# A two-layer convolution and attention trunk: the issue order of every engine written out in traced order

## The chip, the cores and the metric

The kernel runs on one core of a Trainium2 chip. The metric is device time in microseconds for one execution of the whole program, and the kernel before has a median of 1953.31 us over 3 runs (1951.56 to 1954.4). In the text PE is the matmul engine, DVE the vector engine, ACT the scalar engine, POOL the GpSimd engine (here it issues DMAs) and SP the engine that issues the weight loads.

## What is computed

There are 256 tokens with 2048 channels, in float32, and two layers. A layer is this:

```python
h = rmsnorm(x, norm_g)
c_a, c_glu, c_gate, q_down, kv_down, k_pe, m_gate, g_conv, g_mla = split(h @ w_in)
u = causal_depthwise_conv(c_a * sigmoid(c_glu), width=31) + conv_b
y_conv = (silu(layernorm(u)) * silu(c_gate)) @ w_proj_conv
q = rmsnorm(q_down) @ w_uq;  kv = rmsnorm(kv_down) @ w_ukv     # 16 heads, QK norm, rotary part
y_mla = (chunk_causal_attention(q, k, v) * silu(m_gate)) @ w_proj_mla
x = x + (sigmoid(g_conv) * y_conv + sigmoid(g_mla) * y_mla) @ w_out
```

## The kernel before, in words

Every dense product takes float32 weights and activations split in a high and a low part. ACT casts the weights to the high part, `hi` (line 198), DVE subtracts it to get the low part, `lo` (line 199), and PE runs three matmuls per tile: hi with the activations' high part, lo with it, hi with their low part (lines 251 to 253). Weights come by SP in pieces of four 128-row tiles (`load`, line 177, three buffers). A piece makes two splits of two tiles each (`split`, line 189, three buffers each for hi and lo). One split feeds 12 matmuls: two token halves, two tiles, three terms. This text calls that stretch of PE work a slot. `product` (line 239) is the loop over the slots of one block of output columns: for slot i it first issues split i+2, then the 12 matmuls, then `background` (line 216). A block has 16 tiles (8 slots) or, for `uq` and `ukv`, 4 tiles (2 slots); it is 512 columns wide, except `down` (384, 384, 320) and `uq` (384).

`order_of_layer` (line 88) sets the order of the blocks: three `down` blocks, two `glu` blocks, then for each of 8 pairs of heads one `uq`, one `ukv` and one `glu` (or `cgate`) block; then `cgate`, `mgate`, `gmla`, `pmla`, `gconv`, `pconv`, `wout`, four blocks each.

Work beside the products: `attention` (line 532) places the steps of a pair of heads a given number of slots ahead (constants at lines 64 and 65). `turn` (line 281) transposes a tile through DRAM: POOL writes it out with four DMAs, fetches it back `FETCH_AFTER` slots later, DVE transposes 32x32 blocks. `conv` (line 703) puts the 31 taps of a channel block on the list `fill`, each two DVE instructions (line 715). `layernorm` (line 727) puts its steps there too: `centre` subtracts the mean and squares, `var` computes the factor 1/sqrt, `apply` multiplies by it on DVE and runs Silu on ACT, `gated` transposes the gate, multiplies, and splits the result (`ycT`) on ACT and DVE. `background` takes from `fill` at a rate; what is left is drained at the first `pconv` block (line 948). The results of `mgate`, `pconv` and `wout` go through `turn` and are split on ACT and DVE too (`oT` lines 826 and 827, `yT` lines 806 and 807, `hT` lines 897 to 900).

What decides the order on each engine: the Tile framework's scheduler, which runs on a timeline of its own. The wrappers `vec`, `act` and `dma` (line 126) pin the order among the instructions issued through them; instructions issued with `nc.vector`, `nc.scalar`, `nc.tensor` and `nc.sync` are free. Splits are issued with a high priority (line 197), and some steps are tied behind the newest split (lines 203 and 580).

Of the kernel before, what the change touches and what calls it, by code (L numbers as in the profile page):

```python
# [2 lines left out]

# [8 lines left out]
F32 = mybir.dt.float32  # L12
# [46 lines left out]
N_WARM = 9  # L59
TURNED_AFTER = 7  # L60
FETCH_AFTER = 4


STATS_AT, QK_OUT_AT, QK_BACK_AT, ROPE_AT, NOPE_AT, SCORES_AT = 1, 4, 8, 13, 14, 17
P_OUT_AT, P_BACK_AT, P_AT, VALUES_AT = 20, 24, 28, 30

SUMS_AFTER = 1
# [20 lines left out]
def order_of_layer():  # L88

    order = [("down", i, "win") for i in range(len(DOWN_BLOCKS))] + [("glu", 0, "win"), ("glu", 1, "win")]  # L90
    for b in range(NPAIR):
        order += [("uq", b, "wuq"), ("ukv", b, "wukv")]
        if b + 2 < 8:
            order.append(("glu", b + 2, "win"))
        elif b + 1 < NPAIR:
            order.append(("cgate", 0, "win"))
    for kind, s in (
        ("cgate", "win"), ("mgate", "win"), ("gmla", "win"), ("pmla", "wpm"),
        ("gconv", "win"), ("pconv", "wpc"), ("wout", "wo"),
    ):  # L100
        order += [(kind, i, s) for i in range(1 if kind == "cgate" else 0, 4)]
    return order
# [11 lines left out]
def trunk(ctx: ExitStack, tc: tile.TileContext, xT, x, g_in, pos, win, wuq, wukv, wpc, wpm, wo, cst, rows, invf, out):  # L114
    nc = tc.nc

    class InOrder:


        def __init__(self, engine):  # L120
            self.engine = engine

        def __getattr__(self, name):
            return lambda *a, **k: tc.keep_in_program_order(getattr(self.engine, name)(*a, **k))  # L124

    vec, act, dma = InOrder(nc.vector), InOrder(nc.scalar), InOrder(nc.gpsimd)
# [45 lines left out]
    loaded, done, newest = {}, {}, [None]  # L172
    deferred = deque()
    LOAD_AHEAD, SPLIT_AHEAD = 2, 2
    SPLIT_SOONER = 100

    def load(i):
        if i >= len(pieces) or i in loaded:
            return
        ap, n = pieces[i]  # L180
        t = raw_p.tile([P, KG, n], F32, tag="raw", name=f"raw{i}")
        step = KS if i == 0 else KG
        for k in range(0, KG, step):
            if i == 0:
                load_x(k // step)
            nc.sync.dma_start(t[:, k : k + step, :], ap[:, k : k + step, :])
        loaded[i] = t

    def split(i):
# [7 lines left out]
        with tc.high_priority(offset=SPLIT_SOONER):  # L197
            nc.scalar.copy(hi, r)  # L198
            ins = nc.vector.tensor_sub(lo, r, hi.bitcast(F32))  # L199
        done[i] = hi, lo  # L200
        newest[0] = ins.ins
        while deferred and deferred[0][0] <= i:
            with tc.issue_after(ins.ins):
                deferred.popleft()[1]()
# [4 lines left out]
    attn, fill = deque(), deque()  # L209
    budget = {"fill": 0.0, "rate": 0.0, "slots": 0}  # L210
    steps, clock = [], [0]

    def at_slot(ahead, f):
        steps.append((clock[0] + ahead, f))

    def background():
        clock[0] += 1
        if attn:
            attn.popleft()()
        due = [f for slot, f in steps if slot <= clock[0]]  # L220
        steps[:] = [e for e in steps if e[0] > clock[0]]
        for f in due:
            f()
        if budget["slots"]:

            budget["rate"] = max(sum(cost for cost, _ in fill), 0.0) / budget["slots"]
            budget["slots"] -= 1
        budget["fill"] = min(budget["fill"] + budget["rate"], 4.0)
        while fill and budget["fill"] > 0:
            cost, f = fill.popleft()  # L230
            budget["fill"] -= cost
            f()

    def drain(q):
        while q:
            f = q.popleft()
            (f[1] if isinstance(f, tuple) else f)()

    def product(planned, stat, evacuate):
        nk, n, mine = planned  # L240
        pts = [acc_p.tile([P, 512], F32, tag="acc", name=f"acc{mine[0]}_{t}") for t in range(T)]
        for j, i in enumerate(mine):
            for a in range(SPLIT_AHEAD + 1):
                split(i + a)
            hi, lo = done[i]
            for t in range(T):
                for kk in range(KS):
# [3 lines left out]
                    nc.tensor.matmul(pts[t][:, :n], sh, hi[:, kk, :], start=first, stop=False)  # L251
                    nc.tensor.matmul(pts[t][:, :n], sh, lo[:, kk, :], start=False, stop=False)  # L252
                    nc.tensor.matmul(pts[t][:, :n], sl, hi[:, kk, :], start=False, stop=last)  # L253
            if j < len(mine) - 1:
                background()
        for t in range(T):
            evacuate(t, pts[t][:, :n])
        background()
# [5 lines left out]
    def park(src, n, home):  # L264
        d = home.tile([4, 32, 4, n // 4], F32, tag=f"t{n}", name="turn_d")
        for i in range(4):
            dma.dma_start(
# [5 lines left out]
    def fetch(d, z):  # L273
        dma.dma_start(z, d.rearrange("j s i e -> (j s) (i e)"))
# [6 lines left out]
    def turn(src, n, use, dst=None):  # L281
# [4 lines left out]
        at_slot(FETCH_AFTER, lambda: back.append(fetched(d, n)))  # L286
# [6 lines left out]
        deferred.append((len(done) - 1 + TURNED_AFTER, blockwise))  # L293
# [24 lines left out]
    nc.vector.memset(ones, 1.0 / D)  # L318
# [7 lines left out]
    nc.vector.memset(zeros.bitcast(F32), 0.0)  # L326
    nc.scalar.copy(sin2[:, 0, 0, :], ones[:, :HALF])
    warm = tp_p.tile([P, 512], F32, tag="tp", name="warm")
    for i in range(N_WARM):
        nc.tensor.matmul(warm, zeros[:, :P], zeros, start=i == 0, stop=i == N_WARM - 1)  # L330

    gains = const.tile([P, DEPTH, NCT], F32, name="gains")
    nc.sync.dma_start(gains, g_in)
    x_in = big.tile([P, NCT, SEQ], F32, tag="big", name="x_in")
    x_chunks = [(0, 2), (2, 4), (4, 8), (8, 12), (12, 16)]

    def load_x(i):
        a, b = x_chunks[i]
        nc.sync.dma_start(x_in[:, a:b, :], xT[:, a:b, :])

    def rope_tables():
        invf_t = const.tile([P, HALF], F32, name="invf_t")
        nc.gpsimd.dma_start(invf_t, invf.partition_broadcast(P))
        pos_t = const.tile([P, T], I32, name="pos_t")
        nc.gpsimd.dma_start(pos_t, pos)
        posf = const.tile([P, T], F32, name="posf")
        nc.vector.tensor_copy(posf, pos_t)
        tables = wide_p.tile([P, 6, T, HALF], F32, tag="w", name="tables")
        ang, ah, al, turn, whole, frac = (tables[:, i] for i in range(6))
        ah = ah.bitcast(F32R)  # L350
        for t in range(T):
            nc.vector.tensor_scalar(ang[:, t, :], invf_t, posf[:, t : t + 1], None, op0=ALU.mult)
        nc.vector.tensor_copy(ah, ang)
        nc.vector.tensor_sub(al, ang, ah.bitcast(F32))
        big_half = 1.5 * 2.0**23

        def reduce_to(dst, src, scale):

            nc.vector.tensor_scalar(whole, src, scale, big_half, op0=ALU.mult, op1=ALU.add)
            nc.vector.tensor_scalar(whole, whole, -big_half, None, op0=ALU.add)  # L360
            nc.vector.scalar_tensor_tensor(dst, src, scale, whole, op0=ALU.mult, op1=ALU.subtract)

        first = True
        for piece in revolution_pieces():
            for a in (ah.bitcast(F32), al):
                reduce_to(turn if first else frac, a, piece)
                if not first:
                    nc.vector.tensor_add(turn, turn, frac)
                first = False
        for dst, shift in ((sin2, 0.0), (cos2, 0.25)):  # L370
            nc.vector.tensor_scalar(frac, turn, shift, None, op0=ALU.add)
            reduce_to(ang, frac, 1.0)
            for h in range(2):
                nc.scalar.activation(dst[:, :, h, :], ang, AF.Sin, scale=2.0 * np.pi)
# [4 lines left out]
    def sum_x():  # L379
        tot = small.tile([P, T], F32, tag="totx", name="totx")  # L380
        nc.vector.reduce_sum(tot, ss_x, axis=AX.X)
# [5 lines left out]
    load(0)  # L387
    for i in range(2, len(x_chunks)):
        load_x(i)
        if i < len(x_chunks) - 1:  # L390
            load(i - 1)
    for c in range(NCT):
        g = gains[:, 0, c : c + 1]
        nc.scalar.activation(h_hi[:, c, :], x_in[:, c, :], AF.Copy, scale=g)
        nc.vector.scalar_tensor_tensor(
            h_lo[:, c, :], x_in[:, c, :], g, h_hi[:, c, :].bitcast(F32), op0=ALU.mult, op1=ALU.subtract
        )

    def first_sums(t, c):
        xt = wide_p.tile([P, 512], F32, tag="w", name="xres")  # L400
        tc.keep_in_program_order(nc.sync.dma_start(xt, x[t, :, c * 512 : (c + 1) * 512]))
        junk = work.tile([P, 512], F32, tag="junk", name="junk")
        nc.scalar.activation(junk, xt, AF.Square, accum_out=ss_x[:, t, c : c + 1])


    for l in range(DEPTH):
# [9 lines left out]
        def load_consts(row=row, C=C, l=l):  # L416
            tc.keep_in_program_order(nc.sync.dma_start(row, rows[l].partition_broadcast(P)))
            tc.keep_in_program_order(nc.sync.dma_start(C, cst[l]))
# [9 lines left out]
        def down_evac(i, t, ps, down=down):  # L428
            at, n = DOWN_BLOCKS[i]
            nc.scalar.activation(down[:, t, at : at + n], ps, AF.Copy, scale=rinv_x[:, t : t + 1])  # L430

        def down_after(down=down, qkc=qkc, ss_d=ss_d, r_d=r_d, kpe=kpe, ccq=ccq, ssq_t=ssq_t, gqk=gqk, row=row, C=C):
            for t in range(T):
                for i, (a, n) in enumerate(((0, LORA), (LORA, LORA), (2 * LORA, ROPE))):
                    junk = work.tile([P, 512], F32, tag="junk", name="junk")
                    nc.scalar.activation(junk[:, :n], down[:, t, a : a + n], AF.Square, accum_out=ss_d[:, i, t : t + 1])
            rms_factor(r_d.rearrange("p a t -> p (a t)"), ss_d[:, 0:2, :].rearrange("p a t -> p (a t)"), LORA)
            for i in range(2):
                for t in range(T):
                    d = down[:, t, i * LORA : (i + 1) * LORA]  # L440
                    nc.vector.scalar_tensor_tensor(
                        d, d, r_d[:, i, t : t + 1], row[:, i * LORA : (i + 1) * LORA], op0=ALU.mult, op1=ALU.mult
                    )
            for c in range(0, 8, 2):
                tp = tp_p.tile([P, 2, SEQ], F32, tag="tp", name="tp_d")
                for j in range(2):
                    for t in range(T):
                        nc.tensor.transpose(
                            tp[:, j, t * P : (t + 1) * P], down[:, t, (c + j) * P : (c + j + 1) * P], ident
                        )  # L450
                nc.scalar.copy(qkc[:, 0, c : c + 2, :], tp)
                nc.vector.tensor_sub(qkc[:, 1, c : c + 2, :], tp, qkc[:, 0, c : c + 2, :].bitcast(F32))

            def gained(dst, table, base):
                g = row[:, base : base + ROPE].unsqueeze(1).broadcast_to([P, T, ROPE])
                nc.vector.tensor_mul(dst, table.rearrange("p t h d -> p t (h d)"), g)
# [599 lines left out]
```

## Time and profile before

| what | value |
| --- | --- |
| the profiled execution's own time | 1953.72 us |
| its span, first to last instruction | 1952.0 us |
| around the span | 1.7 us |
| median of the three timed runs | 1953.31 us |
| DMA | 437.58 MB, mean 224 GB/s |
| ACT busy | 1111.4 us (57%) |
| POOL busy | 363.0 us (19%) |

In a row of a group the columns are: line, engine, operation, names out<-in, shapes, count; then busy time and mean length of one in ns; then the idle time of the engine just before them and what ended it. In a timeline row: start, length, engine, line, operation, names, shape, count, and in brackets the engine's idle time before it. A length counts until the result has left the pipeline, so two independent instructions on one engine start a little closer together than a length.

### The profile page before, as it was taken

The page shows a single profiled execution, that of the slowest core. Times are in us where ns is not written, and L with a number is a line of the kernel's source. Part 1 is how long each engine was busy: PE and PEld are TensorE (multiplying, and loading weights), DVE is VectorE, ACT ScalarE, POOL GpSimd, SP SyncE. Part 2 cuts the span into 40 slices and gives each one's busy share as a digit, 9 for nine tenths or more (in the row PEclk, how much of TensorE's full clock was granted, in tenths as well). Part 3 has the DMA queues.
Part 4 walks back from the last instruction along what each step waited for, and adds up shares of the span by engine and source line. Part 5 has one row for each costly group of instructions (what it writes and reads, how often), then busy time and mean ns, then how long its engine had stood idle before and what let it go on. Part 6 is the DMA issues. An engine that isn't in the chain of part 4 may idle for free.

```text
span 1952.0 us, 25418 instructions
## 1 busy us (share of the span) xinstructions
PE 1910.5 (98%) x8781; PEld 1607.7 (82%) x8781; DVE 1614.0 (83%) x2884; ACT 1111.4 (57%) x1778; POOL 363.0 (19%) x684
## 2 busy tenths in 40 slices
PE   9999999999999999999999999999999999999998
PEld 8888877788888888788898887877888888887886
DVE  7688889789999998865656888887999999987654
ACT  6556777666554445644555677766655444456442
POOL 0123322422210000021201323333323000001200
PEclk9999999999999999999999999999999999999999
DMA  7667765676765556576765676567767555555764
GB/s 288 220 217 256 248 210 197 233 245 243 260 216 194 194 194 221 194 238 242 272 221 203 247 251 237 190 225 251 242 239 246 215 194 194 193 208 216 240 211 161
DMA packets 85650, 437.58 MB, mean 224 GB/s; under 512 B 16896, under 2 KB 19984, under 8 KB 46608
## 3 DMA queue, kind: packets, MB, share of 16 engines
q1 hardware_dynamic: 55728, 361.44, 51.8%
q0 software_dynamic: 29792, 74.51, 11.8%
q8 instruction: 69, 1.13, 0.2%
q14 instruction: 61, 0.50, 0.1%
HBM read 395.51 MB, written 40.37 MB: 223 GB/s over the span
## 4 chain that ended last, share of the span: by engine, by line
PE 85%; DVE 6%; DMA 4%; ACT 2%; issue 2%; POOL 1%; SPq 0%; DVEq 0%; ACTq 0%; POOLq 0%
PE acc L252 27%; PE acc L251 27%; PE acc L253 27%; DVE v_t L124 2%; DVE lo L199 1%; DMA turn_d<-qk 1%; PE o_ps L664 1%; ACT hi L198 1%; DMA qk<-turn_d 1%; POOL turn_d L124 1%; PE s L625 1%; DMA turned<-turn_d 1%; DVE qk_t L124 1%; ACT qk_t L124 1%; DVE turned L124 0%
## 5 line engine op out<-in xcount | busy, mean ns | idle before, releaser
L198 ACT CAST hi<-raw 128x1024 fp32r<-128x1024 f32 (+2 forms) x688 | 704.4, 1026 | 735.3 <-PE acc L253 535.7
L199 DVE TENSOR_TENSOR lo<-raw,hi 128x1024 fp32r<-128x1024 f32 (+2 forms) x688 | 815.0, 1185 | 267.5 <-ACT hi L198 265.4
L124 DVE SCALAR_TENSOR_TENSOR v_t<-u_t,cst,v_t 128x256 f32<-128x256 f32 x960 | 411.8, 476 | 2.8 <-ACT v_t L124 2.5
L252 PE MATMUL acc<-lo,h_hi 128*128 128x512 f32 (+2 forms) x864 | 333.1, 386 | 2.2 <-DVE lo L199 2.2
L252 PE MATMUL acc<-lo,hT 128*128 128x512 f32 (+2 forms) x864 | 331.4, 384 | 2.4 <-DVE lo L199 2.4
L253 PE MATMUL acc<-hi,h_lo 128*128 128x512 f32 (+2 forms) x864 | 331.7, 384 | 0.0
L253 PE MATMUL acc<-hi,hT 128*128 128x512 f32 (+2 forms) x864 | 330.1, 383 | 0.0
L251 PE MATMUL acc<-hi,h_hi 128*128 128x512 f32 (+2 forms) x864 | 299.9, 385 | 3.5 <-ACT hi L198 2.8
L251 PE MATMUL acc<-hi,hT 128*128 128x512 f32 (+2 forms) x864 | 298.2, 383 | 0.6 <-ACT junk L511 0.6
L252 PEld LDWEIGHTS acc<-lo,h_hi 128*128 128x128 f32 x864 | 163.5, 189 | 33.9 <-DVE lo L199 4.2
L251 PEld LDWEIGHTS acc<-hi,h_hi 128*128 128x128 f32 x864 | 163.2, 190 | 34.1 <-ACT hi L198 3.5
L252 PEld LDWEIGHTS acc<-lo,hT 128*128 128x128 f32 x864 | 162.5, 188 | 33.7 <-DVE lo L199 4.2
L253 PEld LDWEIGHTS acc<-hi,h_lo 128*128 128x128 f32 x864 | 163.5, 189 | 29.6
L251 PEld LDWEIGHTS acc<-hi,hT 128*128 128x128 f32 x864 | 161.9, 188 | 30.5 <-ACT junk L511 0.8
L253 PEld LDWEIGHTS acc<-hi,hT 128*128 128x128 f32 x864 | 162.3, 188 | 29.5
L124 POOL DMA_DIRECT2D turn_d<-gate x176 | 95.8, 551 | 168.2 <-DVE gate L874 105.9
L124 POOL DMA_DIRECT2D turn_d<-qk x128 | 69.7, 552 | 272.1 <-DVE qk L124 226.1
L124 POOL DMA_DIRECT2D turn_d<-su x128 | 69.8, 552 | 268.5 <-DVE su L696 199.7
L124 POOL DMA_DIRECT2D turned<-turn_d x82 | 44.7, 547 | 388.9 <-DVE ln_stats L124 271.7
L252 PE MATMUL acc<-lo,ycT 128*128 128x512 f32 x256 | 99.5, 390 | 1.3 <-DVE lo L199 1.3
L253 PE MATMUL acc<-hi,ycT 128*128 128x512 f32 x256 | 99.5, 390 | 0.9 <-DVE ycT L124 0.9
L252 PE MATMUL acc<-lo,yT 128*128 128x512 f32 x256 | 99.9, 390 | 0.4 <-DVE lo L199 0.4
(196 smaller groups left out, 2701.8 us busy)
## 6 DMA issues: line engine op xcount, KB each, us to landing
raw<-in_win SPq DMA_DIRECT2D x192, 1024.0 KB, 5.0
raw<-in_wpm SPq DMA_DIRECT2D x32, 1024.0 KB, 4.8
raw<-in_wpc SPq DMA_DIRECT2D x32, 1024.0 KB, 4.9
raw<-in_wo SPq DMA_DIRECT2D x32, 1024.0 KB, 5.1
raw<-in_wukv SPq DMA_DIRECT2D x16, 1024.0 KB, 6.6
turned<-turn_d POOLq DMA_DIRECT2D x50, 256.0 KB, 4.8
raw<-in_wuq SPq DMA_DIRECT2D x16, 768.0 KB, 4.4
turn_d<-qk POOLq DMA_DIRECT2D x128, 96.0 KB, 4.2
```

Source lines behind the costliest of these rows:

```text
L124: return lambda *a, **k: tc.keep_in_program_order(getattr(self.engine, name)(*a, **k))
L198: nc.scalar.copy(hi, r)
L199: ins = nc.vector.tensor_sub(lo, r, hi.bitcast(F32))
L251: nc.tensor.matmul(pts[t][:, :n], sh, hi[:, kk, :], start=first, stop=False)
L252: nc.tensor.matmul(pts[t][:, :n], sh, lo[:, kk, :], start=False, stop=False)
L253: nc.tensor.matmul(pts[t][:, :n], sl, hi[:, kk, :], start=False, stop=last)
L625: nc.tensor.matmul(s1[:, h, :], qa, ka, start=n == 0, stop=n == len(terms) - 1)
L664: nc.tensor.matmul(o_ps[:, h, kt * P :], v[j][:, kt, h, :], pt[i][:, h, queries], start=n == 0, stop=n == len(todo) - 1,)
```

## The change

1. `vec`, `act` and the new `pe`, `gps`, `sp` chain each instruction to the one before it on its engine, so that all five engines issue in the order in which the program is traced. No instruction is free any more, and the priorities and `deferred` are gone.
2. Every step sits in a slot. `at_slot` takes a cost in DVE microseconds; `background` counts, per slot, the matmuls' time less that of `lo`, subtracts the costs of the steps due, and takes from `fill` while something is left. A block's evacuation comes one slot after its last matmuls; a turned tile is transposed 8 slots after it was sent. `background(s)` is traced behind split s+2 and ahead of split s+3, on every engine.
3. The first `glu` block comes ahead of `down`, `glu` runs one pair further ahead, and two `cgate` blocks stand among the pairs.
4. Once the last pair's `ukv` is done, every other tap is taken in part by ACT: it scales the shifted block (two instructions) and DVE adds both halves in one.
5. At the start the first piece comes in steps of 1, 1 and 2 tiles, the gains come on ACT's queue, and there are 11 warming matmuls instead of 9. At the end the residual is loaded when a `wout` block begins (`wout_begin`), and the last block is written in halves on two queues.

```diff
-N_WARM = 9
-TURNED_AFTER = 7
-FETCH_AFTER = 4
+FIRST_STEPS = ((0, 1), (1, 2), (2, 4))
+N_WARM = 11
+EVAC_AT = 1
+FETCH_AT, TURNED_AT = 4, 8
...
         def __getattr__(self, name):
-            return lambda *a, **k: tc.keep_in_program_order(getattr(self.engine, name)(*a, **k))
-
-    vec, act, dma = InOrder(nc.vector), InOrder(nc.scalar), InOrder(nc.gpsimd)
+            def issue(*a, **k):
+                ins = getattr(self.engine, name)(*a, **k)
+                if self.last is not None:
+                    order = mybir.DependencyInfo(mybir.DependencyClass.NoSync, mybir.DependencyReason.DATA)
+                    tc.add_manual_dep(ins.ins, self.last.name, order, reason="order of issue")
+                self.last = ins.ins
+                return ins
+
+            return issue
+
+    pe, vec, act, gps, sp = (InOrder(e) for e in (nc.tensor, nc.vector, nc.scalar, nc.gpsimd, nc.sync))
...
+    def background(n):
         clock[0] += 1
...
+        budget["us"] = min(budget["us"], 0.0) + 12 * (n / 2400 + 0.0133) - (KS * n / 960 + 0.06) - 0.04
+        while True:
+            due = [e for e in steps if e[0] <= clock[0]]
+            if not due:
+                break
+            steps[:] = [e for e in steps if e[0] > clock[0]]
+            for _, cost, f in due:
+                budget["us"] -= cost
+                f()
+        while fill and budget["us"] > 0 and clock[0] >= budget["hold"]:
+            run_fill()
...
+            if j == len(mine) - 1:
+                steps.insert(0, (clock[0] + 1 + evac_at, cost, evac))
+            background(n)
...
+            def scale(k):
+                scaled[k] = wide_p.tile([P, 2, SEQ], F32, tag="w", name="tap")
+                for j in range(2):
+                    act.activation(scaled[k][:, j, :], us[b][:, j, k : k + SEQ], AF.Copy, scale=weight(k, j))
...
+                elif k in scaled:
+                    vec.tensor_add(v[:, :, :SEQ], v[:, :, :SEQ], scaled.pop(k))
+                    cost = 0.6
...
+                    if budget["assist"] and k + 1 < CONV_W:
+                        scale(k + 1)
...
             for b in range(8):
-                fill.append((0.7, lambda b=b: apply(b)))
+                fill.append((1.1, lambda b=b: apply(b), 0))
...
+        def wout_begin(c, keep=keep, l=l):
+            for t in range(T):
+                keep["x", c, t] = wide_p.tile([P, 512], F32, tag="w", name="xres")
+                sp.dma_start(keep["x", c, t], (x if l == 0 else x1_dram)[t, :, c * 512 : (c + 1) * 512])
```

More of the change, by code (lines that the diff above doesn't have):

```diff
@@ L100, in order_of_layer @@
     ):
-        order += [(kind, i, s) for i in range(1 if kind == "cgate" else 0, 4)]
+        order += [(kind, i, s) for i in range(2 if kind == "cgate" else 0, 4)]
     return order
@@ L200, in split @@
         done[i] = hi, lo
[L201 to L204, printed above, removed]
         for a in range(1, LOAD_AHEAD + 1):
             load(piece + a)
-    attn, fill = deque(), deque()
-    budget = {"fill": 0.0, "rate": 0.0, "slots": 0}
     steps, clock = [], [0]
-    def at_slot(ahead, f):
-        steps.append((clock[0] + ahead, f))
-    def background():
+    fill, budget = deque(), {"us": 0.0, "hold": 0, "assist": False}
@@ L217, in background, with at_slot @@
+    def at_slot(ahead, f, cost=0.0):
+        steps.append((clock[0] + ahead, cost, f))
+    def background(n):
         clock[0] += 1
[L218 to L228, printed above, removed]
@@ L250, in product @@
                     first, last = k == 0, k == nk - 1
[L251 to L258, printed above, removed]
+                    pe.matmul(pts[t][:, :n], sh, hi[:, kk, :], start=first, stop=False)
+                    pe.matmul(pts[t][:, :n], sh, lo[:, kk, :], start=False, stop=False)
+                    pe.matmul(pts[t][:, :n], sl, hi[:, kk, :], start=False, stop=last)
+            if j == len(mine) - 1:
+                steps.insert(0, (clock[0] + 1 + evac_at, cost, evac))
+            background(n)
     def stat_of(hi, lo):
@@ L386, in trunk, with first_h, begin, end @@
     h_lo = big.tile([P, NCT, SEQ], F32R, tag="big", name="h_lo")
+    def first_h(c):
+        g = gains[:, 0, c : c + 1]
+        act.activation(h_hi[:, c, :], x_in[:, c, :], AF.Copy, scale=g)
+        vec.scalar_tensor_tensor(
+            h_lo[:, c, :], x_in[:, c, :], g, h_hi[:, c, :].bitcast(F32), op0=ALU.mult, op1=ALU.subtract
+        )
     load(0)
-    for i in range(2, len(x_chunks)):
+    for i in range(3, len(x_chunks)):
         load_x(i)
         if i < len(x_chunks) - 1:
[L391 to L397, printed above, removed]
-    def first_sums(t, c):
[L400 to L403, printed above, removed]
+            load(i - 2)
+    def first_sums(t, c):
+        xts = []
+        def begin():
+            for a in (c, c + 1):
+                xts.append(wide_p.tile([P, 512], F32, tag="w", name="xres"))
+                sp.dma_start(xts[-1], x[t, :, a * 512 : (a + 1) * 512])
+        def end():
+            for a, xt in zip((c, c + 1), xts):
+                junk = work.tile([P, 512], F32, tag="junk", name="junk")
+                act.activation(junk, xt, AF.Square, accum_out=ss_x[:, t, a : a + 1])
+        return begin, end
     for l in range(DEPTH):
@@ L429, in down_evac @@
             at, n = DOWN_BLOCKS[i]
-            nc.scalar.activation(down[:, t, at : at + n], ps, AF.Copy, scale=rinv_x[:, t : t + 1])
+            act.activation(down[:, t, at : at + n], ps, AF.Copy, scale=rinv_x[:, t : t + 1])
         def down_after(down=down, qkc=qkc, ss_d=ss_d, r_d=r_d, kpe=kpe, ccq=ccq, ssq_t=ssq_t, gqk=gqk, row=row, C=C):
[L433 to L456, printed above, removed]
-            gained(ccq, cos2, R_KR)
-            gained(ssq_t, sin2, R_KR)
             ka = work.tile([P, T, ROPE], F32, tag="qa", name="ka")
@@ L577, in blockwise @@
             def blockwise():
-                for t in range(T):
-                    z = p["qk"][:, t].rearrange("p j i c -> p (j i c)")
-                    with tc.issue_after(newest[0]):
-                        vec.transpose(z, z)
+                for z in rows:
+                    vec.transpose(z, z)
             def split_nope(which):
@@ L763, in apply @@
                     )
-            fill.append((0.8, mean))
-            for b in range(8):
-                fill.append((1.2, lambda b=b: centre(b)))
             gates = {}
@@ L953, in trunk @@
+                while i == 0 and "yc" not in keep:
+                    run_fill()
+                product(pl, stat_of(*keep["yc"]), lambda t, ps, i=i: pconv_evac(i, t, ps), cost=2.4, before=before)
+            else:
+                wout_begin(i)
+                last = last_layer and i == 3
+                product(pl, stat_of(*keep["y"]), lambda t, ps, i=i, f=wout_evac: f(i, t, ps), 0 if last else EVAC_AT, 1.25)
         if not last_layer:
```

580 lines of the change are left out of this document (334 added, 246 removed).

## The prediction

> **What bounds it now.** I read the totals first, then the split's windows by stage, then PE's waits.
>
> ```profile
> span 1952.0 us, 25418 instructions
> PE 1910.5 (98%) x8781; PEld 1607.7 (82%) x8781; DVE 1614.0 (83%) x2884; ACT 1111.4 (57%) x1778; POOL 363.0 (19%) x684
> ```
>
> PE is 98% busy, so nothing but its matmuls, its few waits and the two ends can set the time. What a gain can reach shows when the stages are set against a slot of PE work. The next fence shows two of the last slots on the three engines, the one behind it the count of splits of the two larger widths.
>
> ```profile
> 1933.69 0.62 PE L251 MATMUL acc<-hi,yT 128*128 128x512 f32 x2
> 1933.89 1.05 ACT L198 CAST hi<-raw 128x1024 fp32r<-128x1024 f32 x1 [1.67 <-PE acc L253]
> 1934.98 1.22 DVE L199 TENSOR_TENSOR lo<-raw,hi 128x1024 fp32r<-128x1024 f32 x1 [1.50 <-ACT hi L198]
> 1936.41 0.62 PE L251 MATMUL acc<-hi,yT 128*128 128x512 f32 x2
> ```
> ```profile
> L199 DVE TENSOR_TENSOR lo<-raw,hi 128x1024 fp32r<-128x1024 f32 x608 | 740.7, 1219 | 220.7 <-ACT hi L198 219.1
> L199 DVE TENSOR_TENSOR lo<-raw,hi 128x768 fp32r<-128x768 f32 x64 | 61.1, 956 | 36.3 <-ACT hi L198 36.0
> ```
>
> A full slot is 1936.41 − 1933.69 = 2.72. `hi` starts 0.20 into it and `lo` ends at 1936.20, 2.51 into it. That split is read two slots later, by the second matmul, at 2 × 2.72 + 0.23 = 5.67. So a split has **3.1 us of lead**; PE stalls for what exceeds it. 608 slots of 2.72, 64 of three quarters of that (2.04) and the 16 left at 1.7 make 1811.6. The stages, by the window and the count of `lo` in it:
>
> ```profile
> 104.00:500.00 396.00, 154.96 (x131) 0.98 0.68 234
> 500.00:772.00 272.00, 121.35 (x101) 1.00 0.59 209
> 772.00:812.00 40.00, 15.74 (x13) 1.00 0.53 184
> 1072.00:1468.00 396.00, 155.61 (x131) 0.98 0.67 234
> 1740.00:1780.00 40.00, 14.76 (x13) 1.00 0.51 188
> ```
> ```profile
> PE s L625 <- ACT qk_t L124: 9.8, 6, 2.2
> PE acc L252 <- DVE lo L199: 6.3, 7, 1.8
> PE acc L251 <- ACT hi L198: 3.8, 3, 2.8
> 169.43 0.22 PE L610 MATMUL s<-qk_t 128*128 128x128 f32 x1
> 170.86 0.34 PE L253 MATMUL acc<-hi,qkc 128*128 128x384 f32 x1
> 500.17 1.30 PE L664 MATMUL o_ps<-pv 128*128 128x128 f32 x10
> 501.32 0.40 PE L252 MATMUL acc<-lo,h_hi 128*128 128x512 f32 x1
> ```
>
> From 500 to 772 there is no wait: 272 us for 100 slots. In an attention stage 131 splits (115 full, 16 of 768 columns) are 345.4. Twelve score matmuls take 170.86 − 169.43 = 1.43 and ten value matmuls 1.15, so a pair's 16 and 12 take 3.25, eight pairs 26. What is left of 396 is about **24 us of waits** per layer. At the `pconv` edge (772, 1740) 13 slots are 35.4 of 40, so 4.6 of waits each. The rest of what is not slots lies at the two ends.
>
> **The change, part by part.** *Attention (order, costs, glu first).* The longest waits there are for score inputs and for `hi` and `lo` behind bursts. The built program places the steps of a pair slot by slot with DVE's time counted, and all that a score matmul reads is made at least one slot ahead. I take 46 of the 48 us away (bounds 30 and 48). *The edge.* The built order empties the list of fill just about where `pconv` starts: −8 of 9.2 (0 to −9.2).
>
> *The two ends.*
>
> ```profile
> 8.62 1.01 PE L251 MATMUL acc<-hi,h_hi 128*128 128x384 f32 x2 [2.82 <-ACT hi L198]
> 1944.35 0.39 PE L253 MATMUL acc<-hi,yT 128*128 128x512 f32 x1
> 1944.75 0.42 SPq L880 DMA_DIRECT2D xres<-x_dram  x1
> 1947.86 0.69 DVE L881 TENSOR_TENSOR xres<-acc,xres 128x512 f32<-128x512 f32 x1 [3.53 <-DMA xres<-x_dram]
> ```
>
> The last add waits 3.53 for a residual that is requested at 1944.75, after the last matmul has started at 1944.35; `wout_begin` requests it a block earlier. The add can then start near 1944.5: −3.4 (−2 to −3.8, two queues included). At the start a first step of one tile lets ACT and DVE begin on less than the first matmul waits 2.82 for now: −2 (0 to −4). Gains together: 46 + 8 + 3.4 + 2 = **−59.4**.
>
> *The strict order.* This is the cost. `background(s)` is traced between split s+2 and split s+3. On ACT `hi` of s+3 therefore stands behind every ACT step of slot s, and `lo` of s+3 behind every DVE step. Where these steps wait for each other in turn, the whole loop is paid, though each engine alone would have room. Before, the scheduler moved `hi` ahead and put steps in blocks, as here in layernorm's `apply`:
>
> ```profile
> 788.41 4.89 DVE L124 TENSOR_TENSOR v_t<-v_t,ln_stats 128x512 f32<-128x512 f32 x8
> 789.18 1.28 ACT L124 ACT_TABLE_LOAD   x1
> 790.47 2.08 ACT L124 ACTIVATE v_t<-v_t,cst 128x256 f32<-128x256 f32 x4
> 777.39 0.42 DVE L124 SCALAR_TENSOR_TENSOR rsq_t<-rsq_t,ln_stats 128x256 f32<-128x256 f32 x1
> 777.85 0.42 DVE L124 SCALAR_TENSOR_TENSOR ln_stats<-rsq_t,ln_stats 128x256 f32<-128x256 f32 x1
> ```
>
> Eight multiplies are 0.61 apart, the last result coming 0.72 after its start; a Silu is 0.5, a table load 1.29. Now the order is `lo`, multiply, two Silus, `hi`, `lo`: 0.72 + 0.99 + 1.09 + 1.14 = 3.94 for a slot of 2.72. The lag grows by 1.22 per such slot, by about 4.0 in slot 272, where two table loads and two gates' activations stand between, and by about 1.6 in the slots of `gated` (multiply, cast, subtract). The factor 1/sqrt is 12 dependent DVE steps 0.46 apart (777.39 to 777.85), about 5.3 in one slot: by itself 0.7 beyond the lead, and the lead is spent when `apply` begins. Five slots at 1.22, slot 272, two `gated` slots and 0.7 give 6.1 + 4.0 + 3.2 + 0.7 = 14.0; with what recovers between, 13.7 for layer one. Layer two is laid out a little worse: 15.7. `centre` (subtract, square, add in turn, +0.75 to +1.95 a slot in seven slots) overshoots by 3.5 per layer. Layernorm: 13.7 + 15.7 + 7 = **+36.4** (bounds +8, if only rsqrt and slot 272 overshoot, and +55, if nothing recovers).
>
> *Evacuation and turned tile in one slot.* Blocks are 8 slots long, evacuated 1 after their end and turned 8 after sending, so both fall on the same slot:
>
> ```profile
> L124 DVE STREAM_TRANSPOSE turned<-turned 128x512 f32<-128x512 f32 x50 | 34.7, 700 | 3.4 <-DMA turned<-turn_d 3.4
> L819 DVE TENSOR_TENSOR gate<-gate,rinv 128x512 f32<-128x512 f32 x16 | 10.8, 682 | 1.1 <-ACT gate L816 1.1
> L124 ACT CAST oT<-o_sb 128x1024 fp32r<-128x1024 f32 x8 | 8.4, 1047 | 0.0
> L806 ACT CAST yT<-turned 128x512 fp32r<-128x512 f32 x12 | 7.4, 619 | 2.1 <-DVE turned L124 2.1
> L124 ACT ACTIVATE hT<-turned,gains 128x128 fp32r<-128x128 f32 x24 | 7.8, 392 | 5.2 <-DVE turned L124 5.1
> ```
>
> In a `mgate` slot (168, 176, 184 and the same in layer two) DVE does two gate products, two transposes and two products from 2.51 on: six steps of 0.61 to 0.64, done near 6.3. Then come the cast (1.05), `hi` and `lo`, to 9.6. Split s+3 is due at 3 × 2.72 + 0.23 less a weight load, 8.27. So +1.3 each, six times, +9 with lag carried in. In a `yT` slot (296, 304, 312 and in layer two) four gate steps, then transpose, cast, subtract twice end `lo` near 10.3: +2.05, six times, +12.3. In an `hT` slot (328, 336, 344, layer one alone) two residual adds, then transpose and eight small steps in turn, twice: +1.83, three times, +5.5. Bounds for the three together: +5 and +35.
>
> *The rest.* Rotary tables at the start +2.5 and the statistics' chain of 13 dependent small steps +4.2, both near the lead's edge (0 to +12). Taps on ACT and more table loads fill ACT's idle 43%; the cover is the slack that the loops above use up, and where it is gone the cost is in the terms above.
>
> ```profile
> 253.62 0.63 PE L251 MATMUL acc<-hi,h_hi 128*128 128x512 f32 x1
> 254.05 0.63 PE L252 MATMUL acc<-lo,h_hi 128*128 128x512 f32 x1
> ...
> 256.18 0.46 PE L251 MATMUL acc<-hi,h_hi 128*128 128x512 f32 x1
> ```
>
> Behind the stall at 253 matmuls stood 0.43 apart instead of 0.23 until 256.18, six steps of 0.2 more. One stall of the new kernel (slot 272, about 4) is as long; I count +2 in both layers together. [...]
>
> The costs are 36.4 + 9 + 12.3 + 5.5 + 6.7 + 2 = 71.9; with the gains −59.4 + 71.9 = **+12.5**. Span 1952.0 + 12.5 = 1964.5, own time with 1.7 around it 1966; the profiled execution stands 0.4 above the median, which is within its spread.
>
> **The rivals.** *Faster.* The loops stay within the lead: links overlap more than I count (a split's lead refills by 1.2 to 1.6 in each lighter slot), and about 15 of the 71.9 remain. Then 1953.7 − 59.4 + 15 = 1909. It is decided by whether the lag in slots 256 to 282 passes 3.1. For it: only a few dozen of 688 slots overshoot; against it: the rows' durations, end to end. A rule of the Trainium skill speaks for my side: "PSUM — Partial Sum Buffer", section "Engine vs sequencer instructions", has ACT's and DVE's queues as strictly first in, first out, so `hi` cannot pass a waiting Silu; with it the sum is +12.5, without it this rival.
>
> *No difference.* The loops cost five sixths of my count, and gain and loss cancel: 1953.
>
> *DVE as the bound, slower still.* Late taps are paced by counted costs.
>
> ```profile
> L124 DVE SCALAR_TENSOR_TENSOR v_t<-u_t,cst,v_t 128x256 f32<-128x256 f32 x960 | 411.8, 476 | 2.8 <-ACT v_t L124 2.5
> ```
>
> Two of these and the dependent add of 512 columns take 0.40 + 0.51 + 0.71 = 1.62 in a row, against 1.41 if independent. If that excess is paid in some 65 slots of both layers beyond the lead (0.21 × 2 × 65 = 28), the time is 1994. Against it: a tap's add can be followed by an independent `lo`. It decides if DVE shows no idle time from slot 190 to 255.
>
> That the order is not what the diff says is excluded by the built program.
>
> **How the numbers follow.** Forecast 1966, range of its own 1955 to 1985, chance 0.58; faster 0.22; no difference 0.12; DVE bound 0.08. About 0.2% (3.9 us) is what can be told from no change. With layernorm at its bounds of 8 and 55 the sum gives 1938 and 1985, with the evacuations at 5 and 35 it gives 1944 and 1974. Range 1926 to 1990: it takes these in and leaves out most of the faster rival and part of the DVE one. Faster 0.22, within 0.2% 0.12, slower 0.66.
>
> **What would show it.** Right: the attention windows of the new trace have almost no PE waits; PE waits for `lo` and `hi` in slots 256 to 282 and once in each `mgate`, `yT` and `hT` slot above, 1 to 4 us long; ACT's idle before `hi` is ended by DVE's `v_t`, `turned` or `o_sb`; the last add starts within 0.3 us of the last matmul. Wrong: layernorm's 26 slots without a wait (then about 1910), or waits spread over the tap stage (then above 1985).

## The result and the profile after

The changed kernel takes 2057.82 us (median of 4 runs, 2055.45 to 2062.2) against 1953.44: 1.0538 times the time before, with an interval of 1.0519 to 1.0558. The profiled execution has a span of 2053.7 us. I forecast 1966 and a range up to 1990: the sign held, the size did not.

First the totals and PE's waits of the changed kernel (a row of waits is: who waited, for whom, us in total, times, longest). All wrapped instructions now have line 128, so names tell them apart.

```profile
span 2053.7 us, 25692 instructions
PE 1945.0 (95%) x8787; PEld 1598.1 (78%) x8787; DVE 1615.7 (79%) x2701; ACT 1248.4 (61%) x2136; POOL 370.9 (18%) x694
```
```profile
PE acc L128 <- DVE lo L128: 62.2, 91, 1.0
PE acc L128 <- ACT hi L128: 39.8, 43, 2.8
```

The waits of the scores, `s L625`, are gone, as forecast. In their place stand 102 us of waits for the splits themselves, on 91 and 43 occasions, the longest 2.8. Where they lie is seen when the span is cut at the first product matmul of a stage: from the start to `mgate`, `mgate`, `gmla` with `pmla` (the tap stage), `gconv` with `pconv`, `wout`, for both layers. The columns are stretch, its length, PE busy (matmuls), the granted clock as a share of full speed, DMA share and GB/s. The first fence is the kernel before, the second the changed one.

```profile
8.62:444.50 435.88, 423.76 (x2025) 0.98 0.68 238
444.50:536.20 91.70, 91.70 (x425) 1.00 0.72 244
536.20:710.30 174.10, 174.10 (x769) 1.00 0.56 200
710.30:889.80 179.50, 176.99 (x775) 1.00 0.62 217
...
978.50:1411.20 432.70, 420.46 (x2034) 0.98 0.65 229
...
1677.00:1856.60 179.60, 177.11 (x776) 1.00 0.60 217
```
```profile
6.35:455.50 449.15, 424.17 (x2025) 0.99 0.68 233
455.50:553.70 98.20, 94.46 (x426) 0.98 0.67 223
553.70:733.10 179.40, 176.25 (x769) 1.00 0.55 190
733.10:933.10 200.00, 184.51 (x777) 0.99 0.58 200
...
1026.90:1476.30 449.40, 426.44 (x2033) 0.98 0.65 220
1476.30:1576.70 100.40, 95.34 (x426) 0.98 0.65 218
1576.70:1756.80 180.10, 176.31 (x769) 1.00 0.54 190
1756.80:1959.50 202.70, 184.34 (x778) 1.00 0.56 198
```

The stage of `down`, `glu` and attention did not get 40 us shorter in both layers together; it got 13.3 and 16.7 longer. `gconv` with `pconv`, where layernorm stands, got 20.5 and 23.1 longer, `mgate` 6.5 and 8.6, the tap stage (`gmla`, `pmla`) 5.3 and 6.1 (layer two of the kernel before has 91.8 and 174.0 there). `wout` got 5.1 and 1.5 longer (93.8 against 88.7, and in layer two, to the last matmul, 89.3 against 87.8).

The mechanism is plainest in layernorm. ACT and DVE of the changed kernel, two turns of the `apply` slots; in brackets the idle time and what ended it:

```profile
805.71 1.23 DVE L128 TENSOR_TENSOR lo<-raw,hi 128x1024 fp32r<-128x1024 f32 x1 [2.48 <-ACT hi L128]
806.85 0.69 DVE L128 TENSOR_TENSOR v_t<-v_t,ln_stats 128x512 f32<-128x512 f32 x1
809.63 1.23 DVE L128 TENSOR_TENSOR lo<-raw,hi 128x1024 fp32r<-128x1024 f32 x1 [2.10 <-ACT hi L128]
```
```profile
807.57 1.09 ACT L128 ACTIVATE v_t<-v_t,cst 128x256 f32<-128x256 f32 x2 [1.90 <-DVE v_t L128]
808.57 1.03 ACT L128 CAST hi<-raw 128x1024 fp32r<-128x1024 f32 x1
811.50 1.09 ACT L128 ACTIVATE v_t<-v_t,cst 128x256 f32<-128x256 f32 x2 [1.90 <-DVE v_t L128]
```

A turn of the loop takes 3.92 (809.63 − 805.71); I had worked out 3.94. Both engines are idle for half of it: ACT waits 1.90 for the multiply, DVE waits 2.10 for `hi`, which stands behind the Silus.

In attention the same loop runs through other steps, which I had not added up. DVE and ACT of one pair of heads, the slots of the rotary casts and of `ukv`'s evacuation:

```profile
285.81 1.83 DVE L128 STREAM_TRANSPOSE qk<-qk 128x768 f32<-128x768 f32 x2
...
291.33 1.23 DVE L128 TENSOR_TENSOR lo<-raw,hi 128x1024 fp32r<-128x1024 f32 x1 [0.77 <-ACT hi L128]
292.47 0.42 DVE L128 TENSOR_TENSOR pv<-acc,pv 128x256 fp32r<-128x256 f32 x1
...
296.72 1.22 DVE L128 TENSOR_TENSOR lo<-raw,hi 128x1024 fp32r<-128x1024 f32 x1 [0.84 <-ACT hi L128]
```
```profile
285.18 1.05 ACT L128 CAST hi<-raw 128x1024 fp32r<-128x1024 f32 x1
287.68 2.54 ACT L128 CAST qk_t<-qk 64x256 fp32r<-64x256 f32 x6 [1.45 <-DVE qk L128]
290.24 1.05 ACT L128 CAST hi<-raw 128x1024 fp32r<-128x1024 f32 x1
...
292.92 0.37 ACT L128 COPY qk<-acc 128x256 f32<-128x256 f32 x1 [1.36 <-DVE pv L128]
...
295.65 1.98 ACT L128 CAST hi<-raw 128x1024 fp32r<-128x1024 f32 x2
```

`hi` starts at 285.18, 290.24 and 295.65: 5.06 and 5.41 apart where a slot takes 2.72. ACT waits for the transposes, casts, then comes `hi`, then `lo`, and behind `lo` the subtraction for which ACT's next copy waits. PE runs out of lead at the end of such a burst:

```profile
296.74 0.50 PE L128 MATMUL acc<-hi,h_hi 128*128 128x512 f32 x1 [1.34 <-ACT hi L128]
298.00 0.50 PE L128 MATMUL acc<-lo,h_hi 128*128 128x512 f32 x1 [0.76 <-DVE lo L128]
...
334.83 0.50 PE L128 MATMUL acc<-hi,h_hi 128*128 128x512 f32 x1 [0.92 <-ACT hi L128]
```

So the waits of attention come as one burst per pair of heads (the next is 38 us later), and between two bursts PE does not wait.

Most of the tap stage's loss is not the taps' either. In layer one its first three waits are these. They stand behind the casts of turned `mgate` tiles, which themselves wait for DVE (one cast is shown):

```profile
560.88 1.05 ACT L128 CAST oT<-o_sb 128x1024 fp32r<-128x1024 f32 x1 [4.81 <-DVE o_sb L128]
562.93 0.50 PE L128 MATMUL acc<-hi,h_hi 128*128 128x512 f32 x1 [0.95 <-ACT hi L128]
564.38 0.50 PE L128 MATMUL acc<-lo,h_hi 128*128 128x512 f32 x1 [0.95 <-DVE lo L128]
587.56 0.50 PE L128 MATMUL acc<-lo,h_hi 128*128 128x512 f32 x1 [0.95 <-DVE lo L128]
```

They make 2.9 of the 3.1 us that PE waits there; the last `mgate` block is evacuated, and the last two are turned, when `gmla` already runs.

### The profile page after: what moved, and what is told of

Its sections match the earlier page's. It is cut to its first block, busy times and chain, and to the rows that moved or that the text cites. A ratio compares the mean times of both kernels' runs of the same rounds, so it can differ in the third digit from the quotient of the medians.

```text
span 2053.7 us, 25692 instructions
## 1 busy us (share of the span) xinstructions
PE 1945.0 (95%) x8787; PEld 1598.1 (78%) x8787; DVE 1615.7 (79%) x2701; ACT 1248.4 (61%) x2136; POOL 370.9 (18%) x694
## 5 line engine op out<-in xcount | busy, mean ns | idle before, releaser
L128 DVE TENSOR_TENSOR lo<-raw,hi 128x1024 fp32r<-128x1024 f32 (+3 forms) x689 | 811.8, 1184 | 336.3 <-ACT hi L128 335.2
L128 ACT CAST hi<-raw 128x1024 fp32r<-128x1024 f32 (+3 forms) x689 | 695.1, 1021 | 486.1 <-PE acc L128 440.0
L128 PE MATMUL acc<-hi,hT 128*128 128x512 f32 (+2 forms) x1728 | 539.6, 389 | 18.2 <-ACT hi L128 18.2
L128 PE MATMUL acc<-lo,h_hi 128*128 128x512 f32 (+2 forms) x864 | 338.1, 391 | 26.6 <-DVE lo L128 26.5
L128 DVE SCALAR_TENSOR_TENSOR v_t<-u_t,cst,v_t 128x256 f32<-128x256 f32 x608 | 263.4, 481 | 4.2 <-ACT v_t L128 0.8
L128 PE MATMUL acc<-hi,yT 128*128 128x512 f32 x512 | 159.6, 390 | 2.0 <-ACT hi L128 2.0
L128 PE MATMUL acc<-hi,oT 128*128 128x512 f32 x512 | 158.3, 390 | 0.0
L128 ACT ACTIVATE tap<-u_t,cst 128x256 f32<-128x256 f32 x352 | 158.2, 501 | 0.0
L128 PE MATMUL acc<-hi,qkc 128*128 128x512 f32 (+1 forms) x512 | 147.3, 363 | 0.0
L128 DVE TENSOR_TENSOR v_t<-v_t,tap 128x512 f32<-128x512 f32 x176 | 121.3, 689 | 12.8 <-ACT tap L128 5.1
L128 PEld LDWEIGHTS acc<-hi,ycT 128*128 128x128 f32 x512 | 96.1, 188 | 27.1 <-ACT hi L128 7.4
```

The source lines that it names most:

```text
L128: ins = getattr(self.engine, name)(*a, **k)
```

## The experiments

Theory A: pinned in traced order, `hi` stands behind ACT steps that wait for DVE, and `lo` waits for `hi`; these loops set the pace of busy slots. I added to it that a fill which pads DVE to the full slot lets no lag recover. Theory B: single bursts pass the lead and the rest recovers. Theory C: DVE has more to do than a slot holds. Times are medians of 2 to 10 executions; the run with fewer taps is a single one.

**`hi` one split earlier.**

```diff
-KG = 4
+KG = 2
...
-    raw_p = pool("raw", 3)
+    raw_p = pool("raw", 5)
...
+    hi_p = pool("hi", 4)
...
-    LOAD_AHEAD, SPLIT_AHEAD = 2, 2
+    LOAD_AHEAD, SPLIT_AHEAD = 4, 2
...
             for a in range(SPLIT_AHEAD + 1):
                 split(i + a)
+            high(i + SPLIT_AHEAD + 1)
```

`high` is new and casts `hi` alone; `lo` is made where it was.

> The changed kernel with the cast hi of split s+3 issued ahead of lo of split s+2, so that on ACT hi of s+3 no longer stands behind the steps of slot s (a fourth hi buffer, paid for by weight pieces of two tiles instead of four). Theory A (loops between ACT and DVE slow every busy slot, and a fill that pads DVE to the full slot lets no lag recover): most of the loop is opened, the 63 to 67 us of waits that the changed kernel has beside the slots in its two attention stages fall to under 30, the time to 1960 to 2000. Theory B (single bursts in single slots pass the lead, the rest recovers): the bursts in layernorm, mgate, yT and hT get shorter by one hi (1 us each), attention hardly changes, 2025 to 2045. Theory C (DVE has simply more to do than a slot holds, pacing too fast): no change, 2045 to 2060.

1953.82 us, 1.0001 times the kernel before (0.9992 to 1.001): all 104 us that the changed kernel had lost come back, a little more than A had it. Its waits, its stages, and DVE in the same `apply` stage:

```profile
PE acc L128 <- DVE lo L128: 38.4, 49, 2.7
...
PE acc L128 <- ACT hi L128: 0.3, 1, 0.3
```
```profile
6.46:434.10 427.64, 416.76 (x2026) 1.00 0.75 245
434.10:531.60 97.50, 93.96 (x426) 0.98 0.73 224
...
709.80:890.60 180.80, 177.78 (x777) 1.00 0.69 221
```
```profile
770.22 1.22 DVE L128 TENSOR_TENSOR lo<-raw,hi 128x1024 fp32r<-128x1024 f32 x1
771.35 1.29 DVE L128 TENSOR_TENSOR v_t<-v_t,ln_stats 128x512 f32<-128x512 f32 x2
772.56 1.22 DVE L128 TENSOR_TENSOR lo<-raw,hi 128x1024 fp32r<-128x1024 f32 x1
```

PE's waits for `hi` fall from 39.8 to 0.3. In layernorm `lo` now follows the multiplies at once, without idle time, and the stage falls from 200.0 to 180.8; the first stage falls from 449.15 to 427.64, now 8 below the kernel before. Nearly all of these 8 is the clock and not the waits: PE is idle for 10.9 of the stage against 12.1 before, but the granted clock is 1.00 against 0.98, and 0.02 × 436 is 8.7 (an estimate). `mgate` hardly moves in this layer; what is left of waits is for `lo` throughout.

**The pieces alone.** The same kernel with `KG = 2` and five buffers, without the earlier cast.

> The changed kernel with the weight pieces of two tiles (five buffers) that paid for the fourth hi buffer, and nothing else of that run. Theory A/B (ACT's hi behind waiting steps is the cause): within 10 us of the changed kernel's 2058, so the 104 us that the earlier cast gave back are its own. Rival (the larger pieces starved the splits or collided with the turns' DMAs): much of the 104 us appears here, below 2010.

2053.71, within 10 as expected: the pieces give 4 of the 104 us, the earlier cast 100.

**The mirror: the kernel before, `hi` pinned.**

```diff
-            nc.scalar.copy(hi, r)
+            act.copy(hi, r)
```

> The kernel before, with one edit: the cast hi is issued through the wrapper that keeps ACT in traced order, so hi stands behind the steps traced ahead of it; lo stays free. If hi behind waiting ACT steps is the cause of the loss, most of it appears here without slots, costs, glu first or late taps on ACT: 1990 to 2060. If it needs the change's slots as well, 1950 to 1970.

2188.51, 1.1206 times the time (1.1185 to 1.1226): a single word costs more than the whole change, and more than the 2060 that I had as the most. That the steps are not spread over slots in this kernel may be the reason; it was not tried.

```profile
PE acc L251 <- ACT hi L124: 125.0, 59, 13.6
```

PE's wait for `hi` goes from 3.8 to 125.0; part of it lies at the start, where the longest is 13.6. The mean granted clock falls from 0.991 to 0.960 as well, so a part of the 236 us is matmuls at half rate behind the waits (more of this in the last section).

**Both pinned.** As above, and `lo` through `vec`.

> The kernel before, with both hi and lo issued through the wrappers that keep ACT and DVE in traced order. By my theory lo adds little to what pinning hi costs, since DVE's steps wait for ACT and not much else: within 20 us of the run with hi alone, 2000 to 2070. If the two pinnings add up, 30 us or more above it.

2232.18: `lo` adds 44, so the two add up. DVE's own order counts too, about a fifth of what `hi` costs; I had said within 20, and 2070 at most.

**Three splits ahead.** `SPLIT_AHEAD = 3`, four buffers of `hi` and `lo`, `KG = 2` with four buffers of pieces.

> The changed kernel with splits made three ahead instead of two (four buffers of hi and lo, paid for by weight pieces of two tiles), so the lead of a split is 5.8 us instead of 3.1; the order of background and splits among themselves is as before. Theory A: attention gains only once per stage, since the loop still takes more than 2.72 us per slot on average and nothing recovers; the single bursts go: 2000 to 2030. Theory B: all stalls but slot 272's are under the new lead: 1925 to 1960. Theory C: as A, 2030 to 2050.

2007.71 (1.0278; 1.0261 to 1.0295), in A's range, but not for A's reason. A lead of 5.8 us instead of 3.1 gives half of what opening the loop gives. The waits for `hi` and `lo` fall from 102 to 31 us; among what keeps the time up is a new wait of the scores, probably because the steps now stand behind one split more:

```profile
PE s L128 <- DVE qk_t L128: 22.0, 28, 1.6
PE acc L128 <- DVE lo L128: 21.5, 32, 1.0
PE acc L128 <- ACT hi L128: 9.7, 15, 2.8
```

**Splits left free.** `hi` and `lo` through `nc.scalar` and `nc.vector` with the former priority, all else in traced order.

> The changed kernel with hi and lo issued outside the chains of ACT and DVE, with the high priority that they had before the change; all else stays in traced order. If the pinning of the splits is the cause (A or B), the scheduler moves hi and lo ahead of waiting steps and the time falls to 1930 to 1975. If the placing of the other steps in slots or the late taps are the cause (C), it stays above 2030.

1995.58: 62 of the 104 come back, less than I said. PE waits 26.2 for `qk_t` at the scores, a wait that the changed kernel does not have; that the scheduler puts splits ahead of steps that PE needs sooner is the likely reason, which I did not trace.

**Fewer taps, paced lower.** This kernel leaves out 11 taps.

```diff
+TAPS_TAKEN = tuple(range(19)) + (CONV_W - 1,)
...
-        budget["us"] = min(budget["us"], 0.0) + 12 * (n / 2400 + 0.0133) - (KS * n / 960 + 0.06) - 0.04
+        budget["us"] = min(budget["us"], 0.0) + 12 * (n / 2400 + 0.0133) - (KS * n / 960 + 0.06) - 0.04 - 0.28
...
-            for k in range(CONV_W):
+            for k in TAPS_TAKEN:
                 fill.append((0.0, lambda k=k: tap(k), 0))
```

> The changed kernel, leaving out 11 of the 31 taps of the convolution, with 0.28 us less DVE time given out per slot, so that the list of fill ends about where it did. Theory A: with 0.28 us per slot for recovering, the waits of the two attention stages fall from 67 us to 15 to 35, layernorm and the evacuation slots stay as they are, in all 2005 to 2025. Theory B: attention as before, 2040 to 2055. Theory C: the waits of attention and of the tap stage fall in proportion to the work, to under 10, 1985 to 2005.

2054.26. Its first stage, to `mgate`, in both layers, and a wait that it has at `pconv`, since the fill ended late:

```profile
5.57:453.20 447.63, 424.53 (x2025) 0.99 0.69 236
1043.20:1488.70 445.50, 423.70 (x2033) 0.99 0.66 224
```
```profile
PE acc L129 <- ACT ycT L129: 20.8, 4, 5.6
```

447.63 and 445.50 against 449.15 and 449.40: 5.4 us in both, nothing like the 30 to 50 of A, though DVE was busy for 31 us less in each (329.8 against 361.2, 327.6 against 358.7). So the second half of A, a full DVE that lets nothing recover, falls, and C with it: the waits of attention hang on the order within a few slots of each pair, not on DVE's load. Here B was right: the bursts pass the lead, and what lies between them recovers. The time in all says less, as it holds the new wait at `pconv`.

**Turned tiles at 7.** `FETCH_AT, TURNED_AT = 4, 7`.

> The changed kernel with turned tiles transposed 7 slots after sending instead of 8, so that in mgate, pconv and wout a block's evacuation and the transposed tile of the block before fall in different slots. The term of my sum: mgate's 14.8 us of waits, 13 around the yT slots and 8 around the hT slots fall to under 10 together, the time by 20 to 30, to 2028 to 2038. Rival (the chain transpose, cast, subtract is too long by itself wherever it stands): under 10 us gained.

2048.09: 9.7 us, just inside the rival. Evacuation and transposed tile no longer meet, but PE still waits at every turned `mgate` tile: transpose, cast and subtract are a loop by themselves.

**`ukv` reordered.**

```diff
             act.copy(p["vh"][:, t], v)
-            vec.tensor_sub(p["vl"][:, t], v, p["vh"][:, t].bitcast(F32))
             act.copy(p["qk"][:, t, :, 2:4, :], k)
+            vec.tensor_sub(p["vl"][:, t], v, p["vh"][:, t].bitcast(F32))
```

> The changed kernel with the evacuation of ukv reordered: for each half ACT casts v, copies k, and only then DVE subtracts for v. Now ACT's copy of k waits for DVE's subtraction (1.36 and 0.49 us in one pair). If this loop is a main part of the burst of each pair, 1 to 1.6 us per pair go, 16 to 25 in all: 2033 to 2042. If the burst is set by another part (the 13 dependent steps of the statistics, the rotary casts), under 8 us: 2050 to 2058.

2053.52: 4 us, so this one loop is not the burst; the next step on ACT, the squares (`junk`), then waits for the subtraction instead, 20.2 us in 24 waits where the copy had waited 23.4 in 24.

**No taps on ACT.** `budget["assist"] = False`.

> The changed kernel with all taps on DVE (the fourth part undone). My theory: the late taps lie in the tap stage, where there are 11 us of waits beside the slots, and take 0.2 to 0.4 us of DVE time per pair away; without them layernorm starts later and ends in a drain at pconv: 2055 to 2080. If the taps on ACT stand in the loop with hi and cost more than they save, it gets faster: 2035 to 2050.

2095.13, 15 us beyond what I expected, in the same direction: the late taps on ACT are worth 37 us. Without them the fill is drained at `pconv`, where PE then waits 62.8 us for `ycT`.

**Three edits together.** The earlier cast, `ukv` reordered, turned tiles at 7.

> The three edits together: hi cast one split earlier (which alone gave 1954), the ukv evacuation reordered, turned tiles at 7. What stays in the first of them is 27 us beside the slots in the attention stages, 9 in mgate and 6 in pconv. If the remaining bursts are the same loops, half of that goes: 1930 to 1942, faster than before. If they are DVE's own load, nothing changes: 1950 to 1956.

1955.51, 1.0014 (1.0004 to 1.0024): nothing gained over the earlier cast alone. What remains is waits for `lo` (39.4 us); so these are not the same loops. Whether they are DVE's load, as the rival has it, this run does not show.

**Earlier cast, steps spread.**

```diff
-QROT_AT, STATS_AT, SCALE_AT, QK_BACK_AT, QK_TURN_AT, ROPE_AT, NOPE_AT = 1, 2, 3, 7, 11, 12, 15
-SCORES_AT, MAX_AT, EXP_AT, P_BACK_AT, P_TURN_AT, P_SPLIT_AT, VALUES_AT, O_AT = 17, 18, 19, 23, 28, 29, 31, 33
+QROT_AT, STATS_AT, SCALE_AT, QK_BACK_AT, QK_TURN_AT, ROPE_AT, NOPE_AT = 1, 2, 3, 7, 11, 12, 16
+SCORES_AT, MAX_AT, EXP_AT, P_BACK_AT, P_TURN_AT, P_SPLIT_AT, VALUES_AT, O_AT = 18, 19, 20, 24, 29, 30, 32, 34
...
-                if l == 0 and i == 1:
+                if l == 0 and i == 0:
                     tables = rope_tables()
                     for a in range(11):
-                        at_slot(a, lambda: next(tables, None), 0.0 if a < 2 else 1.6)
+                        at_slot(a + a // 2, lambda: next(tables, None), 0.0 if a < 2 else 1.6)
```

> The changed kernel with hi cast one split earlier (1954), the steps of a pair of heads spread over ten slots of twelve instead of eight (nope split at 16, scores 18, maxima 19, exponentials 20, transposed p at 29, its split at 30, values 32, outputs 34), and the rotary tables begun a block earlier. What that kernel still waits is 27 us in attention and 7 at the tables, on lo alone. If DVE's work of eight slots in a row is the cause, half goes: 1932 to 1944, faster than the kernel before. If not, 1950 to 1956.

1947.56, 0.9972 times the kernel before (0.9961 to 0.9984): the only version that beats both, the kernel before by 0.3%, and less than I said. PE's waits for `lo` went from 38.4 only to 33.5, so DVE's eight slots in a row are not shown to be their cause, which stays open. Against the kernel before it has no fewer waits (PE waits 38.8 us in all, 34.2 before); it has the higher clock, 0.999 against 0.991, which is some 16 us (an estimate from the two clocks).

## Why the prediction was wrong

**The step that failed** is *Attention*: "I take 46 of the 48 us away (bounds 30 and 48)". Its reason, that all that a score matmul reads is made a slot ahead, held: no wait of the scores is left. But I asked only what the scores wait for, and apart from the statistics (in the +6.7) I did not ask of these slots what I asked of layernorm's: what stands between `lo` of one split and `lo` of the next. With the +6.7 I had the two first stages at 46 − 6.7 = 39 us shorter; they are 30 longer. That is 69 of the 89 us between 1964.5 and 2053.7. Even my bound of 30 excluded a loss, and no reason in the text did so. The 48 were misread besides: the granted clock in these windows was 0.98, so about 8 of each layer's 24 us (0.02 × 396, an estimate) were matmuls at half rate and no waits.

| stage, both layers | forecast, us | measured, us |
| --- | --- | --- |
| start to `mgate` | −39.3 | +30.0 |
| `mgate` and tap stage | +9 | +26.5 |
| `gconv` with `pconv` | +38.6 | +43.6 |
| `wout` | +9.6 | +6.6 |
| the two ends | −5.4 | −5.0 |
| sum | +12.5 | +101.7 |

**Layernorm, yT, hT, edge.** The mechanism and the size were right: turn by turn 3.92 against 3.94. For `gconv` with `pconv` my terms give +38.6 (36.4 − 8, two thirds of yT's 12.3, and 2 for matmuls at half rate), the traces +43.6. For `wout` they give +9.6 (hT, and the rest of yT), against 5.1 and 1.5.

**mgate** is the second term that was too small: with the tap stage, where its last tiles are turned, 26.5 (15.1 and 11.4) instead of 9. I counted three slots per layer at 1.3. Four overshoot, since each of the four blocks is turned (ACT waits for `o_sb` before all eight casts of `oT`, 32.9 us in all), and PE waits 0.92 to 2.62 us at each of them. Two stretches at half rate fall into the two `mgate` stages (clock 0.98) and cost some 3 us more.

**The taps themselves** cost little. I had them at nothing, and at 28 us in a rival. Of the 11.4 us of the tap stage (5.3 and 6.1), about 7.7 lie at the turned `mgate` tiles, where matmuls stand farther apart than their 0.23, so some 4 are left.

**The ends** were right. The first and the last product matmul of the changed kernel:

```profile
6.35 0.40 PE L128 MATMUL acc<-hi,h_hi 128*128 128x512 f32 x1
2048.76 0.39 PE L128 MATMUL acc<-hi,yT 128*128 128x512 f32 x1
```

The first starts 2.27 us earlier, and the span goes on for 2053.7 − 2048.76 = 4.94 after the last instead of 7.65: −5.0, where −5.4 was forecast.

**The rivals.** "Faster" fell: in layernorm, `pconv` and `wout` PE waited about as computed, in `mgate` longer. That the strict order is what costs is shown by the two opposite runs: opening the loop gives 100 us back, pinning `hi` alone in the kernel before costs 236. The rule of the Trainium skill that I weighed ("PSUM — Partial Sum Buffer", section "Engine vs sequencer instructions": ACT's and DVE's queues are strictly first in, first out) agrees with both, and with the rows above, where `hi` at 808.57 comes behind the Silus. The DVE rival rested on DVE's load. Its sign did not come: DVE was busy for 172.1 of the tap stage's 179.4 us, so it had idle time, and the run with fewer taps speaks against load as a cause.

The range ended at 1990 because I let each cost vary by itself, while most of them had one cause that I had looked for in half of the places only. Two small slips in the working change nothing: split s+3 less a weight load of 0.19 is due at 8.20 and not 8.27, and 0.21 × 2 × 65 is 27.

## What to carry to other kernels

When the order of an engine is fixed, walk the slots and add up the cross-engine chain from one instance of the critical step to the next, in every stage that has such chains, and not only in the one that looks dangerous. Costs counted for one engine alone do not see such a chain. The cure is to issue the step that PE waits for ahead of the steps that wait (one more buffer, worth 100 us here); one split more of lead over the same loop gave half of it.

## What was not expected of the hardware

ACT's copy of `k` starts when DVE's subtraction for `v` has ended (292.47 + 0.42 = 292.89, start 292.92), though both only read one accumulator tile and write different ones. When the copy went ahead, the squares behind it waited in the same way. The profile finds who ended a wait from semaphores, and it names the subtraction, so it is the built program that asks for this order. Whether the chip needs it was not tried.

A short wait can cost twice, since behind some of them matmuls run at half rate for a while. In the kernel before:

```profile
326.73 0.44 PE L664 MATMUL o_ps<-pv 128*128 128x256 f32 x2 [1.08 <-ACT pv L124]
```
```profile
328.00:331.40 3.40, 3.40 (x13) 0.50 0.65 263
```

No wait in the 70 us ahead of this stretch is longer than 1.08 us, and the clock is at half for 3.4 us all the same. Behind the wait of 1.63 us at 341.74 it stays full. So the length of a single wait does not decide it; what does was not tried. The mean granted clock is 0.991 in the kernel before, 0.992 in the changed one and 0.999 with the earlier cast. One minus the clock, times the span, gives some 17, 17 and 2 us (an estimate, high where PE idles in such a stretch). My term of +2 for half rate in the changed kernel was therefore far too small for the whole of it, but the kernel before paid as much already; only the runs with the earlier cast were rid of it.
